# Moving a triangular inverse into the recurrence of a hybrid DeltaNet block, and re-laying its multipliers

## The chip, the cores and the metric

The kernel runs on one core of one Trainium2 chip. The metric is the device time of one execution in microseconds; the time before is the median of three runs. One execution was also recorded by the profiler.

## The reference

One layer of a bidirectional encoder block on 512 tokens of 1024 features in float32. What matters here is the gated DeltaNet branch and, at its edge, the rotary keys of the attention branch:

```python
def chunk_gated_delta_rule(q, k, v, g, beta):      # 8 heads of 128, chunks of 64
    ...
    lower = jnp.where(strict, jnp.einsum('bhnik,bhnjk->bhnij', k_beta, kc) * decay, 0.0)
    t_inv = lax.linalg.triangular_solve(eye + lower, ...)      # inverse of a unit lower triangle, 64 x 64
    u = t_inv @ v_beta
    w = t_inv @ (k_beta * jnp.exp(gc)[..., None])
    ...
    def step(state, xs):
        v_new = u_i - w_i @ state
        o_i = qd_i @ state + intra_i @ v_new
        state = state * jnp.exp(gl_i)[..., None, None] + jnp.swapaxes(ks_i, -1, -2) @ v_new
        return state, o_i
    _, o = lax.scan(step, state0, xs)

qkv = silu(conv(h @ w_in[:, :3072]))               # then heads, q and k normalised
o = o_fwd + o_bwd                                  # the rule once on the sequence, once on it reversed
k_rope = apply_rope(k_r, cos, sin)                 # k_r: 64 features shared by all attention heads
```

The block also has latent attention, a gated merge, an output projection, and an expert-choice mixture of 16 experts, of whose weights the second half of the time is spent streaming.

## The kernel before, in words

Float32 products are made on TensorE from halves: `split` (line 98) lets ScalarE round a tile to a high half, and VectorE or GpSimd subtracts it to get the low half; three matmuls of 128x512 then stand for one product. `lo_engine` (line 141) gives every `lo_n[0]`-th weight tile's low half to VectorE and the others to GpSimd: every third at first, every sixth in the value projection, every second in the recurrence. A projection tile has 24 such matmuls.

A scheduler fixes the order of instructions on each engine at compile time, from the order in which the code is written and from its own costs; every engine then runs its queue in that order and waits where an operand is missing.

The part of the program that the change touches runs like this:

1. *Latent projections and rotary keys* (lines 286 to 410). TensorE projects `kr_ps` (64 rotary features and 32 gate columns), ScalarE copies it to `kr1`, and a product with two identities doubles the 64 rows to 128 (`twice`). Sums of squares of the latent queries (`ones` against `sqs`) are copied to `rs`, transposed, and give the softmax scale `scq`. `rope` rotates the doubled keys: high half `rx`, low half `rl`, a permutation by TensorE into `pT`.
2. *Key and query projection*, then for four token tiles the decay matrices and the chunk products `gkq`; these give the strict triangles `nA` for both types of pass (ty 0 and 1).
3. *Inverses* (line 772). For each type, eight 32x32 diagonal blocks per lane set are gathered by way of memory (`nd_d`), one matrix per partition. `nl` holds the multipliers, `T` (named lanT in the trace) the inverse. Row i needs one multiply of i x i elements into `pr` (line 791) and one reduction (line 792), both on VectorE, for i from 1 to 31. The multipliers of a row are a column of `nl`: `n3[:, 0:i, i]`, a stride of 32 elements. Four copies then order the result (lines 794 to 797) and two stores send it to memory (`td_d`, `tt_d`).
4. *Value projection* (lines 801 to 811). Eight tiles (h = 0 to 7), alternating two PSUM banks `pja` and `pjb`, each followed by a filler tile of the output gates (PSUM tile `mm`). Of each value tile VectorE makes a convolution of four operations (lines 666 and 668), ScalarE the silu into `sl` (tile sq), and TensorE four transposes (`to_tok`, line 674, PSUM tile `tok`). The first inverse is written ahead of this loop; the second, which is written in step 2, is drawn up into it by the scheduler.
5. *Recurrence* (lines 816 to 950): eight steps of both directions at once, steps 0 to 3 with ty 0, steps 4 to 7 with ty 1. `level(s + 1)` loads the next step's blocks (`Tbd`, `TtC`, `vtok`, `ktok`, `kq`) through SP's queue and completes the 64x64 inverse with small corner products (`I<-TtC,Mb`, `I<-Tbd,Qb`). `step(s)` has for each group g of four heads the products Y and Q of the state, the subtraction of Y from `vtok` (line 900), the product V with the inverse, its scaling into `vtok` (line 915, VectorE), the state update S (line 933), and the output (lines 940 to 945). What is left of the 24 filler tiles fills TensorE in and behind the steps.
6. *Mixing* (from line 1005): norms of the outputs, transposes `oT`, output projections; then the experts.

Step 2 of the recurrence starts the second inverse in the code:

```python
for s in range(8):
    if s == 2:
        inverses(1)
    Ln = level(s + 1) if s < 7 else None
    step(s, L)
```

Of the kernel before, what the change touches and what calls it, by code (L numbers as in the profile page):

```python
# [14 lines left out]
OP = mybir.AluOpType  # L15
# [25 lines left out]
def block_kernel(ctx: ExitStack, tc: tile.TileContext, x, c, positions, w_mod, b_mod, g_mix, w_in, conv_w,  # L41
# [41 lines left out]
    def bank(name, bufs=2, reg=None):  # L83

        return (reg or pmm)(name if reg else "mm", 512, bufs=bufs)
# [25 lines left out]
    ident = cst("ident", 128)  # L111
# [232 lines left out]
    for i in range(2):  # L344
        dve.tensor_copy(twice[:64, 64 * i:64 * i + 64], ident[:64, :64])
    kr_ps = bank("kr")
    mm(kr_ps, twice[:64], kr1[:64])
    ss = lat[0]
# [5 lines left out]
    for t in range(4):  # L354
        pe.transpose(ss[:, 128 * t:128 * t + 128], rs[:, 128 * t:128 * t + 128], ident)
    scq = mp("scq", 4)
# [4 lines left out]
    p0.close()  # L361
    pm = Region("pmla", space=PSUM)

    pos_i = mp("pos_i", 1024, I32, tag="qn", bufs=2)[:, :512]
# [411 lines left out]
    def inverses(ty):  # L776
        nl, pr, T = lan("nl", 1024), lan("pr", 1024), lan("lanT", 1024)
        for l0, r0, th, c0 in blocks(ty):
            sp.dma_start(lanes_ap(nd_d[ty], l0),
                         nA[ty][th][r0:r0 + 32].rearrange("p (th n) -> p th n", n=64)[:, :, c0:c0 + 32])  # L780
        sp.dma_start(pr, nd_d[ty])
        dve.tensor_copy(nl[0:64], pr[0:64])
        dve.tensor_copy(nl[64:128], pr[64:128][:, ::-1])
        pool.memset(T, 0.0)
        pool.memset(T[:, 0:1024:33], 1.0)
        sq3 = lambda v: v.rearrange("p (a b) -> p a b", a=32)
        T3, n3 = sq3(T), sq3(nl)
        for i in range(1, 32):
            pv = pr[:, :i * i].rearrange("p (a b) -> p a b", a=i)
            nb = n3[:, 0:i, i][:, None, :].to_broadcast([128, i, i])  # L790
            dve.tensor_tensor(pv, T3[:, 0:i, 0:i], nb, op=OP.mult)  # L791
            dve.tensor_reduce(T3[:, 0:i, i], pv, axis=AX.X, op=OP.add)  # L792
        To, Tt = pr, nl
        dve.tensor_copy(To[0:64], T[0:64])
        dve.tensor_copy(To[64:128], T[64:128][:, ::-1])
        dve.tensor_copy(sq3(Tt)[0:64], T3[0:64].rearrange("p a b -> p b a"))
        dve.tensor_copy(sq3(Tt)[64:128], T3[64:128].rearrange("p a b -> p b a")[:, ::-1, ::-1])
        sp.dma_start(td_d[ty], To)
        sp.dma_start(tt_d[ty], Tt)

    inverses(0)
    lo_n[0] = 6
    for h, ps in proj_tiles(range(2048, 3072, 256), to=lambda n: bank(n, 1, pp_)):
        sl = dp("sq", 512, bufs=4)
        for _ in range(0):
            next(mod_g, None)
        conv(ps, 16 + h, halves(sl))
        to_tok(sl, 1, h, ssq_k[:, :, h])
        for _ in range(FV):
            next(fill_g)  # L810
    pp_.close()
    wm.close()
# [70 lines left out]
    def step(s, L):  # L883
# [24 lines left out]
        for g in range(2):  # L908
# [4 lines left out]
            if s < 7:  # L913
                v_ = vtok[:, hs, :]
                dve.tensor_tensor(v_, pV, bt[:, ty, t, hs][:, :, None].to_broadcast([128, 4, 128]), op=OP.mult)
            vn = dp("vn", [4, 128], bufs=2)
            for h in range(4):
                act.activation(vn[:, h, :], pV[:, h, :], AF.Copy, scale=col(beta, 4 * g + h))
            vns.append(vn)
        for g in range(2):  # L920
            if s < 7:
# [12 lines left out]
        for g in range(2):  # L934
# [8 lines left out]
            else:  # L943
                dve.tensor_tensor(Qs[g], pI, Qs[g], op=OP.add)
                pool.tensor_tensor(oo, oo, Qs[g], op=OP.add)

    L = level(0)
    for s in range(8):
        if s == 2:
            inverses(1)  # L950
        Ln = level(s + 1) if s < 7 else None
        step(s, L)
        L = Ln
# [712 lines left out]
```

## Time and profile before

| what | value |
|---|---|
| median of three runs | 1320.24 us (1316.88 to 1322.08) |
| the profiled execution | 1318.83 us, span 1316.9 us |
| busy: TensorE / VectorE / ScalarE / GpSimd | 1232.7 (94%) / 683.2 (52%) / 473.9 (36%) / 307.7 us (23%) |
| mean granted TensorE clock | 0.974 |
| the chain that ended last | TensorE 67%, VectorE 18% (multiplies of line 791: 4%, reductions of line 792: 2%), DMA 6% |
| multiplies of line 791 | 62, 59.1 us |

The busy share is an average over stages. The time of one stage is read from the waits and timelines of that stage; a span is 1.9 us shorter than the execution's time. In the rows PE is TensorE, PEld its weight loads, DVE VectorE, ACT ScalarE, POOL GpSimd, SP the engine that issues most loads. Two matmul records may stand for one float32 matmul of small operands.

### The profile page before, as it was taken

The page shows a single profiled execution, that of the slowest core. Times are in us where ns is not written, and L with a number is a line of the kernel's source. Part 1 is how long each engine was busy: PE and PEld are TensorE (multiplying, and loading weights), DVE is VectorE, ACT ScalarE, POOL GpSimd, SP SyncE. Part 2 cuts the span into 40 slices and gives each one's busy share as a digit, 9 for nine tenths or more (in the row PEclk, how much of TensorE's full clock was granted, in tenths as well). Part 3 has the DMA queues.
Part 4 walks back from the last instruction along what each step waited for, and adds up shares of the span by engine and source line. Part 5 has one row for each costly group of instructions (what it writes and reads, how often), then busy time and mean ns, then how long its engine had stood idle before and what let it go on. Part 6 is the DMA issues. An engine that isn't in the chain of part 4 may idle for free.

```text
span 1316.9 us, 18274 instructions
## 1 busy us (share of the span) xinstructions
PE 1232.7 (94%) x6911; PEld 773.7 (59%) x6911; DVE 683.2 (52%) x1312; ACT 473.9 (36%) x986; POOL 307.7 (23%) x258
## 2 busy tenths in 40 slices
PE   5999999999997889999999999699999999999895
PEld 2767777666676666878877777443433343343233
DVE  4577777475779895535576766511321312222125
ACT  4355655456543334444542226520210120120103
POOL 2221210332542352434222242300300020020003
PEclk9989999999998988999999999799999999999998
DMA  9421222754363557767479682699999999999995
GB/s 347 123 62 41 77 84 71 229 172 142 121 184 98 167 138 205 217 201 214 161 238 339 215 323 113 254 372 420 420 421 420 421 419 420 421 421 420 421 415 191
DMA packets 153842, 333.82 MB, mean 253 GB/s; under 512 B 44864, under 2 KB 104462, under 8 KB 128794
## 3 DMA queue, kind: packets, MB, share of 16 engines
q1 hardware_dynamic: 130048, 308.75, 63.7%
q10 hardware_dynamic: 23370, 23.50, 5.7%
q8 instruction: 54, 0.88, 0.3%
q0 software_dynamic: 336, 0.41, 0.2%
q14 instruction: 34, 0.28, 0.1%
HBM read 308.42 MB, written 24.20 MB: 253 GB/s over the span
## 4 chain that ended last, share of the span: by engine, by line
PE 67%; DVE 18%; DMA 6%; ACT 3%; issue 2%; POOL 1%; DVEq 0%; ACTq 0%; POOLq 0%; SPq 0%
PE mm L88 23%; PE wg L88 8%; PE dnp L88 7%; PE wu L88 7%; DVE pr L791 4%; PE po L88 4%; DMA exw<-in_w_down_dram 3%; PE sc L88 3%; DVE lanT L792 2%; PE s L88 2%; PE I L88 2%; DMA exw<-in_w_gate_dram 2%; PE S L88 1%; DVE cv L666 1%; DVE cv L668 1%
## 5 line engine op out<-in xcount | busy, mean ns | idle before, releaser
L88 PE MATMUL mm<-hT,wh 128*128 128x512 f32 (+1 forms) x656 | 219.0, 411 | 1.5 <-DVE cv L668 0.7
L96 POOL TENSOR_TENSOR wl<-wraw,wh 128x512 fp32r<-128x512 f32 (+1 forms) x82 | 117.5, 1448 | 289.8 <-ACT wh L99 252.5
L88 PEld LDWEIGHTS mm<-hT,wh 128*128 128x128 f32 (+1 forms) x656 | 123.6, 192 | 40.8 <-issue 8.8
L99 ACT ACTIVATE wh<-wraw 128x512 fp32r<-128x512 f32 (+1 forms) x138 | 86.5, 649 | 141.6 <-PE mm L88 75.5
L88 PE MATMUL mm<-hT,wl 128*128 128x512 f32 (+1 forms) x328 | 132.7, 405 | 0.0
L88 PE MATMUL wg<-exw,xe 128*64 128x512 f32 x512 | 121.2, 600 | 2.9 <-DMA exw<-in_w_gate_dram 1.6
L88 PE MATMUL wu<-exw,xe 128*64 128x512 f32 x512 | 119.2, 605 | 1.3 <-DMA exw<-in_w_up_dram 1.3
L96 POOL TENSOR_TENSOR xl<-xs,xh 128x512 fp32r<-128x512 f32 x32 | 40.3, 1275 | 308.2 <-ACT xh L1366 308.2
L1523 DVE TENSOR_TENSOR ye<-dnp,gt 64x512 f32<-64x512 f32 x30 | 20.7, 689 | 133.4 <-PE dnp L88 117.4
L1464 DVE TENSOR_TENSOR xa<-sc,xa 128x512 f32<-128x512 f32 x56 | 38.5, 691 | 87.7 <-PE sc L88 87.7
L88 PEld LDWEIGHTS wu<-exw,xe 128*64 128x64 f32 x512 | 35.3, 138 | 65.5 <-issue 59.4
L88 PEld LDWEIGHTS mm<-hT,wl 128*128 128x128 f32 (+1 forms) x328 | 62.7, 191 | 16.5 <-issue 1.9
L88 PEld LDWEIGHTS wg<-exw,xe 128*64 128x64 f32 x512 | 33.5, 136 | 64.0 <-issue 54.7
L791 DVE TENSOR_TENSOR pr<-lanT,nl 128x1 f32<-128x1 f32 (+30 forms) x62 | 59.1, 953 | 1.7
L96 DVE TENSOR_TENSOR wl<-wraw,wh 128x512 fp32r<-128x512 f32 (+2 forms) x56 | 45.0, 811 | 25.3 <-ACT wh L99 25.1
L88 PE MATMUL po<-W,am 128*128 128x512 f32 x192 | 50.4, 406 | 0.8 <-DVE W L96 0.6
L88 PE MATMUL mm<-am,wh 128*128 128x512 f32 x128 | 41.2, 399 | 0.0
L88 PEld LDWEIGHTS po<-W,am 128*128 128x128 f32 x192 | 34.4, 188 | 11.1 <-issue 1.6
L666 DVE SCALAR_TENSOR_TENSOR cv<-mm,vecT,cv 128x510 f32<-128x510 f32 (+1 forms) x32 | 23.8, 744 | 33.0 <-ACT cv L662 32.7
L88 PE MATMUL mm<-oz,wh 128*128 128x512 f32 x128 | 40.5, 398 | 0.2 <-ACT wh L99 0.2
L1589 POOL TENSOR_TENSOR xa<-xa,late 128x256 f32<-128x256 f32 (+1 forms) x16 | 10.7, 707 | 123.8 <-DMA late<-in_g_final_dram 123.8
L88 PE MATMUL mm<-OG,xh 128*128 128x256 f32 x128 | 34.2, 304 | 2.8 <-DVE OG L1375 2.8
(597 smaller groups left out, 2407.2 us busy)
## 6 DMA issues: line engine op xcount, KB each, us to landing
exw<-in_w_gate_dram SPq DMA_DIRECT2D x64, 1024.0 KB
exw<-in_w_up_dram SPq DMA_DIRECT2D x64, 1024.0 KB
exw<-in_w_down_dram SPq DMA_DIRECT2D x63, 1024.0 KB
wraw<-in_w_in_dram SPq DMA_DIRECT2D x38, 512.0 KB
wm<-in_w_mod_dram SPq DMA_DIRECT2D x32, 512.0 KB
wraw<-in_w_in_dram ACTq DMA_DIRECT2D x16, 512.0 KB
xa<-in_w_mod_dram SPq DMA_DIRECT2D x16, 512.0 KB
kq<-kq_d SPq DMA_DIRECT2D x7, 1024.0 KB
```

The lines of the kernel that those rows point to most:

```text
L88: return pe.matmul(o, lhsT, rhs, start=start, stop=stop)
L96: eng.tensor_tensor(o, a, b, op=OP.subtract)
L99: act.activation(hi, src, AF.Copy)
L666: dve.scalar_tensor_tensor(cv[:, -s:], ps[:, :512 + s], w(d), cv[:, -s:], op0=OP.mult, op1=OP.add)
L668: dve.scalar_tensor_tensor(cv[:, :512 - s], ps[:, s:], w(d), cv[:, :512 - s], op0=OP.mult, op1=OP.add)
L791: dve.tensor_tensor(pv, T3[:, 0:i, 0:i], nb, op=OP.mult)
L792: dve.tensor_reduce(T3[:, 0:i, i], pv, axis=AX.X, op=OP.add)
L1464: dve.tensor_tensor(y[t][:, c:c + 512], ps, y[t][:, c:c + 512], op=OP.add)
L1523: dve.tensor_tensor(ye[o_, c], ps[64 * q:64 * q + 64, :], gt2[64 * q:64 * q + 64, c], op=OP.mult)
L1589: pool.tensor_tensor(y[t][:, cs], y[t][:, cs], gfin[:, cs], op=OP.mult)
```

## The change

- The multipliers are transposed when they are copied into `nl`, so that row i reads `n3[:, i, 0:i]`, contiguous elements. The reversed half of the lanes is reversed in both directions.
- `inverses` becomes a generator that yields after every row. The first is run through at its old place. The second is run to row 12 ahead of level 0 and then in six portions, one behind each group's `vtok` scaling in steps 0, 1 and 2: to rows 17, 20, 23, 26, 29 and the end.
- The transposes of value tile h are written after the convolution of tile h + 1.
- In the value projection `lo_n[0]` is 1000 instead of 6: GpSimd makes all low halves of weights there.
- The doubling of the rotary keys is put behind the transposes of the sums of squares.

```diff
-    kr_ps = bank("kr")
-    mm(kr_ps, twice[:64], kr1[:64])
     ss = lat[0]
     for i in range(4):
         mm(ss[32 * i:32 * i + 32], ones[:, 0:32], sqs[:, i])
...
     for t in range(4):
-        pe.transpose(ss[:, 128 * t:128 * t + 128], rs[:, 128 * t:128 * t + 128], ident)
+        turned_ = pe.transpose(ss[:, 128 * t:128 * t + 128], rs[:, 128 * t:128 * t + 128], ident)
...
     pm = Region("pmla", space=PSUM)
+    kr_ps = bank("kr")
+    with tc.issue_after(turned_.ins):
+        mm(kr_ps, twice[:64], kr1[:64])
...
         sp.dma_start(pr, nd_d[ty])
-        dve.tensor_copy(nl[0:64], pr[0:64])
-        dve.tensor_copy(nl[64:128], pr[64:128][:, ::-1])
+        sq3 = lambda v: v.rearrange("p (a b) -> p a b", a=32)
+        flip = lambda v: sq3(v).rearrange("p a b -> p b a")
+        dve.tensor_copy(sq3(nl)[0:64], flip(pr)[0:64])
+        dve.tensor_copy(sq3(nl)[64:128], flip(pr)[64:128][:, ::-1, ::-1])
...
         for i in range(1, 32):
             pv = pr[:, :i * i].rearrange("p (a b) -> p a b", a=i)
-            nb = n3[:, 0:i, i][:, None, :].to_broadcast([128, i, i])
+            nb = n3[:, i, 0:i][:, None, :].to_broadcast([128, i, i])
             dve.tensor_tensor(pv, T3[:, 0:i, 0:i], nb, op=OP.mult)
             dve.tensor_reduce(T3[:, 0:i, i], pv, axis=AX.X, op=OP.add)
+            yield i
...
         sp.dma_start(tt_d[ty], Tt)
+        yield 32
 
-    inverses(0)
-    lo_n[0] = 6
+    for _ in inverses(0):
+        pass
+    lo_n[0] = 1000
+    turn = []
     for h, ps in proj_tiles(range(2048, 3072, 256), to=lambda n: bank(n, 1, pp_)):
...
         conv(ps, 16 + h, halves(sl))
-        to_tok(sl, 1, h, ssq_k[:, :, h])
         for _ in range(FV):
             next(fill_g)
+        turn.append((sl, 1, h, ssq_k[:, :, h]))
+        if h:
+            to_tok(*turn[h - 1])
+    to_tok(*turn[7])
...
-                dve.tensor_tensor(v_, pV, bt[:, ty, t, hs][:, :, None].to_broadcast([128, 4, 128]), op=OP.mult)
+                done = dve.tensor_tensor(v_, pV, bt[:, ty, t, hs][:, :, None].to_broadcast([128, 4, 128]), op=OP.mult)
...
             vns.append(vn)
+            if s < 3:
+                with tc.issue_after(done.ins):
+                    upto_i(INV[s][g])
...
+    INV, inv = ((17, 20), (23, 26), (29, 32)), inverses(1)
+
+    def upto_i(n):
+        while next(inv) < n:
+            pass
+
+    upto_i(12)
     L = level(0)
     for s in range(8):
-        if s == 2:
-            inverses(1)
         Ln = level(s + 1) if s < 7 else None
```

TensorE's queue in the value projection before, where tile 4 (pja_3720) begins; tok_3665 from sq_3656 are the transposes of tile 3:

```order
L88 MATMUL mm_3682<-hT7_103,wh_3676 128x512 x2
L88 MATMUL mm_3682<-hT7_103,wl_3677 128x512
L88 MATMUL pja_3720<-hT0_96,wh_3714 128x512 x2
L88 MATMUL pja_3720<-hT0_96,wl_3715 128x512
L88 MATMUL pja_3720<-hT1_97,wh_3714 128x512 x2
L88 MATMUL pja_3720<-hT1_97,wl_3715 128x512
L88 MATMUL pja_3720<-hT2_98,wh_3714 128x512 x2
L674 MATMUL tok_3665<-ident_77,sq_3656 128x128 x4
L88 MATMUL pja_3720<-hT2_98,wl_3715 128x512
```

The same transposes in the changed kernel, tok_3781 from sq_3645; mm_3753 is the filler behind tile 4, and pjb_3798 is tile 5:

```order
L88 MATMUL mm_3753<-hT6_102,wl_3748 128x512
L88 MATMUL mm_3753<-hT7_103,wh_3747 128x512 x2
L88 MATMUL mm_3753<-hT7_103,wl_3748 128x512
L675 MATMUL tok_3781<-ident_77,sq_3645 128x128 x4
L88 MATMUL pjb_3798<-hT0_96,wh_3792 128x512 x2
L88 MATMUL pjb_3798<-hT0_96,wl_3793 128x512
```

The transposes of tile 3 moved from the eighth matmul of tile 4 to the end of the filler behind tile 4.

VectorE's queue before, from the end of the second inverse to step 2 of the recurrence:

```order
L797 COPY nl<-lanT 64x1024
L96 TENSOR_TENSOR wl<-wraw,wh 128x512 x2
L915 TENSOR_TENSOR vtok<-V,bt 128x512 x2
L900 SCALAR_TENSOR_TENSOR vtok<-Y,negc,vtok 128x128 x8
L915 TENSOR_TENSOR vtok<-V,bt 128x512 x2
L933 TENSOR_TENSOR Sst<-Sst,S 128x4x128 x4
L942 TENSOR_TENSOR o_2024<-I,o_2024 128x512 x2
```

VectorE's queue now, from the second `vtok` scaling of step 1 on; pr and lanT are the second inverse:

```order
L924 TENSOR_TENSOR vtok<-V,bt 128x512
L793 TENSOR_TENSOR pr<-lanT,nl 128x529
L945 TENSOR_TENSOR Sst<-Sst,S 128x4x128
L794 TENSOR_REDUCE lanT<-pr 128x23
L945 TENSOR_TENSOR Sst<-Sst,S 128x4x128
L793 TENSOR_TENSOR pr<-lanT,nl 128x576
L945 TENSOR_TENSOR Sst<-Sst,S 128x4x128
L794 TENSOR_REDUCE lanT<-pr 128x24
L945 TENSOR_TENSOR Sst<-Sst,S 128x4x128
L793 TENSOR_TENSOR pr<-lanT,nl 128x625
L954 TENSOR_TENSOR o_2024<-I,o_2024 128x512
L794 TENSOR_REDUCE lanT<-pr 128x25
```

The multiplies and reductions of rows 13 to 31, which stood in one run ahead of the steps, now alternate with the state additions of steps 0 to 2.

TensorE's queue at the rotary keys before, and then now:

```order
L88 MATMUL lat_107<-sqs,ones 32x512
L88 MATMUL mm<-kr_616,twice 128x512
L88 MATMUL lat_107<-sqs,ones 32x512 x3
L88 MATMUL mm<-cq_492,uqh 128x512 x2
L88 MATMUL mm<-cq_492,uql 128x512
```

```order
L88 MATMUL lat_107<-sqs,ones 32x512 x4
L353 MATMUL lat_108<-ident,rs 128x128 x4
L88 MATMUL mm<-kr_616,twice 128x512
L88 MATMUL mm<-cq_492,uqh 128x512 x2
L88 MATMUL mm<-cq_492,uql 128x512
```

The doubling moved behind the other three sums and the four transposes of `rs`, which stood some eleven matmuls later.

## Rows read from the trace of the kernel before

**Rows 1.** Busy times by stretch: engines' busy us (instructions), granted clock, DMA share, GB/s.
```profile
374.10:507.50 133.40, 116.39 (x569) 91.39 (x568) 121.55 (x173) 51.13 (x117) 54.05 (x42) 0.94 0.52 150
507.50:528.00 20.50, 17.49 (x181) 13.94 (x179) 6.25 (x11) 10.07 (x28) 3.59 (x5) 0.83 0.80 225
528.00:636.00 108.00, 106.45 (x1291) 87.86 (x1290) 49.09 (x108) 49.98 (x169) 46.03 (x39) 1.00 0.68 197
```

**Rows 2.** Waits of TensorE from 360 to 520: total us, times, longest.
```profile
PE tok L674 <- ACT sq L669: 16.1, 5, 4.8
PE S L88 <- DVE vtok L915: 2.9, 1, 2.9
```

**Rows 3.** Timeline of TensorE, value projection: start, us, instruction, idle before and its releaser.
```profile
418.03 1.12 PE L674 MATMUL tok<-ident,sq 128*128 128x128 f32 x4 [3.65 <-ACT sq L669]
...
419.37 1.05 PE L88 MATMUL pja<-hT,wh 128*128 128x512 f32 x2
...
454.64 0.63 PE L88 MATMUL mm<-hT,wh 128*128 128x512 f32 x2
...
455.35 0.63 PE L88 MATMUL mm<-hT,wh 128*128 128x512 f32 x2
```

**Rows 4.** Timeline of VectorE, both inverses.
```profile
438.43 1.99 DVE L791 TENSOR_TENSOR pr<-lanT,nl 128x961 f32<-128x961 f32 x1
...
447.89 0.68 DVE L96 TENSOR_TENSOR wl<-wraw,wh 128x512 fp32r<-128x512 f32 x1
...
502.40 3.01 DVE L791 TENSOR_TENSOR pr<-lanT,nl 128x961 f32<-128x961 f32 x1
505.45 1.16 DVE L792 TENSOR_REDUCE lanT<-pr 128x31 f32<-128x961 f32 x1
...
508.14 1.21 DVE L796 COPY nl<-lanT 64x1024 f32<-64x1024 f32 x1
```

**Rows 5.** Groups of VectorE's instructions by line, 374 to 528: busy us, mean ns, idle before.
```profile
L791 DVE TENSOR_TENSOR pr<-lanT,nl 128x1 f32<-128x1 f32 (+30 forms) x62 | 59.1, 953 | 1.7
L792 DVE TENSOR_REDUCE lanT<-pr 128x1 f32<-128x1 f32 (+30 forms) x62 | 31.2, 502 | 1.7
```

**Rows 6.** Timeline of VectorE, end of the first inverse, start of the second.
```profile
445.28 1.12 DVE L797 COPY nl<-lanT 64x1024 f32<-64x1024 f32 x1
...
450.98 0.68 DVE L782 COPY nl<-pr 64x1024 f32<-64x1024 f32 x1 [1.15 <-DMA pr<-nd]
```

**Rows 7.** Timeline of GpSimd around 502.
```profile
500.74 2.89 POOL L96 TENSOR_TENSOR wl<-wraw,wh 128x512 fp32r<-128x512 f32 x2 [10.11 <-ACT wh L99]
```

**Rows 8.** The page's groups: a ScalarE pass of 512 columns, busy us, mean ns.
```profile
L99 ACT ACTIVATE wh<-wraw 128x512 fp32r<-128x512 f32 (+1 forms) x138 | 86.5, 649 | 141.6 <-PE mm L88 75.5
```

**Rows 9.** Groups of VectorE's instructions in the steps, 505 to 640.
```profile
L900 DVE SCALAR_TENSOR_TENSOR vtok<-Y,negc,vtok 128x128 f32<-128x128 f32 x56 | 15.8, 344 | 23.5 <-PE Y L88 23.1 <-DMA Tbd<-td 0.3
L933 DVE TENSOR_TENSOR Sst<-Sst,S 128x512 f32<-128x512 f32 x24 | 15.5, 684 | 8.3 <-PE S L88 8.2
```

**Rows 10.** Timeline of TensorE: the first V of steps 1 and 3.
```profile
527.96 0.94 PE L88 MATMUL V<-vtok,Tbd 128*128 128x128 f32 x6
...
558.77 0.71 PE L88 MATMUL V<-vtok,Tbd 128*128 128x128 f32 x4
```

**Rows 11.** Timeline of VectorE behind the steps.
```profile
635.89 0.69 DVE L944 TENSOR_TENSOR Qs<-I,Qs 128x512 f32<-128x512 f32 x1 [1.38 <-POOL o L945]
...
646.73 1.60 DVE L96 TENSOR_TENSOR am<-a__6088,am 128x512 fp32r<-128x512 f32 x1 [5.52 <-ACT am L99]
...
667.06 1.22 DVE L1040 TENSOR_TENSOR o<-o,ssq 128x1024 f32<-128x1024 f32 x1
```

**Rows 12.** Timeline of TensorE behind the steps.
```profile
672.62 1.03 PE L1045 MATMUL oT<-ident,o 128*128 128x128 f32 x8
```

**Rows 13.** Timeline of TensorE at the rotary keys.
```profile
78.86 2.07 PE L88 MATMUL mm<-kr,twice 64*128 64x512 f32 x2 [2.32 <-ACT kr L340]
```

**Rows 14.** Waits of SP's queue, 440 to 545: total us, times, longest.
```profile
SPq L836 <- DMA z_d<-zz: 27.1, 2, 16.3
```

More of the change, by code (lines that the diff above doesn't have):

```diff
@@ L781, in inverses @@
         sp.dma_start(pr, nd_d[ty])
-        dve.tensor_copy(nl[0:64], pr[0:64])
-        dve.tensor_copy(nl[64:128], pr[64:128][:, ::-1])
+        sq3 = lambda v: v.rearrange("p (a b) -> p a b", a=32)
+        flip = lambda v: sq3(v).rearrange("p a b -> p b a")
+        dve.tensor_copy(sq3(nl)[0:64], flip(pr)[0:64])
+        dve.tensor_copy(sq3(nl)[64:128], flip(pr)[64:128][:, ::-1, ::-1])
         pool.memset(T, 0.0)
         pool.memset(T[:, 0:1024:33], 1.0)
-        sq3 = lambda v: v.rearrange("p (a b) -> p a b", a=32)
         T3, n3 = sq3(T), sq3(nl)
```

## The prediction, made before the result was known

> **What bounds the kernel now.** I read busy times by stretch first. From 374.1 us, where the value projection's second tile starts, to 528.0, where step 1 of the recurrence begins, TensorE idles 17.0 + 3.0 us while VectorE is busy 121.6 of the first 133.4; from 528 to 636 TensorE idles only 1.6 of 108 and VectorE is less than half busy [rows 1]. So the cover is in the steps and the shortage in the value projection. TensorE's waits there have one name: 16.1 us in five waits of the value transposes for the silu, and 2.9 us of step 0's state product S for vtok, queued on VectorE behind the second inverse [rows 2]. Its timeline shows that a wait costs more than itself: after the wait of 3.65 us a pair of 512-wide matmuls takes 1.05 us instead of 0.63, the lower level of the granted clock (1.2 instead of 2.4 GHz) [rows 3]. The mean granted clock was 0.94 and 0.83 in the two stretches: (1 - 0.94) x 133.4 + (1 - 0.83) x 20.5 = 11.5 us at most. **The ceiling of the gain is 20.0 + 11.5 = 31.5 us.** TensorE was full in the next stretch, so time saved here is passed on.
>
> **Contiguous multipliers.** A multiply of 961 elements whose second operand strides by 32 takes 1.99 us; the reduction over the same count takes 1.16, and a two-input subtraction of contiguous operands 0.68 for 512, which is 1.28 for 961 [rows 4]. So the stride costs 0.71 to 0.83 us in 961, or 0.74 to 0.86 ns an element. One inverse multiplies 1 + 4 + ... + 961 = 10,416 elements: 7.7 to 9.0 us less; I take 8.3 (28% of the 59.1 / 2 = 29.6 us that one inverse's multiplies take [rows 5]). Against it stand two copies that now transpose: 1.21 instead of 0.68 each [rows 4, 6], 1.0 us. Four low-half subtractions of 0.68 [rows 4], which overlap a little, leave VectorE between 384 and 450: 2.5 us. VectorE thus passes the point it reached at 449.8 about 9.8 us earlier, near 440. GpSimd takes them at 1.45 us [rows 7]; one tile gives it two, 2.9 us per 5.6 us of TensorE, so it keeps up.
>
> **Value transposes a tile later.** Three matmuls start 0.71 us after one another's three, so one is 0.235 us [rows 3]. By the queue, the transposes of tile 3 stood 32 matmuls behind the tile's last one, 7.5 us; now it is 72, 16.9 us. The same 9 to 11 us of slack come to tiles 2 to 6; the longest wait is 4.8 [rows 2]. Only tile 7 keeps its place: 34 matmuls before, 35 now. Whether it waits depends on VectorE. If TensorE loses nothing, the queue puts tile 6's transposes at 374.1 + 80.8 = 454.9 and tile 7's at 457.8. VectorE finishes the first inverse's copies about 437; the second inverse's load lands 4.5 us later, as it did (446.4 to 451.0 [rows 6]), at 441.5. Then come two copies (2.3), rows 1 to 8 of the inverse with tile 6's convolution (7.3, to 451.1), rows to 12 and tile 7's convolution (4.4, to 455.5). Two silu passes of about 0.65 us [rows 8] end at 452.4 and 456.8, before 454.9 and 457.8. The margin at tile 7 is 1.0 us; one multiply that meets GpSimd costs as much (below). I leave 1 us (0 to 4).
>
> **The second inverse in the steps.** Rows 13 to 31 now stand on VectorE behind vtok of steps 0 to 2. By reductions of the trace (15.6 us for 31 rows [rows 5], 13 of them for rows 13 to 31) and multiplies at the contiguous price, portions are 7.7 us in step 0, 9.3 in step 1, and 10.8 plus four copies of 3.8 in step 2. In step 0 ScalarE copies the states, and only vtok needs VectorE. Steps 1 and 2 decide. One step's own work on VectorE is eight scaled subtractions at 0.28, two vtok products, four state additions and two output additions at 0.64 to 0.69 [rows 9]: 7.6 us, and 1.3 of low halves. Two steps with 9.3 and 14.6 us of inverse make 41.7. TensorE took 30.8 us from V of step 1 to V of step 3 [rows 10]; its queue now holds 60 projection matmuls there instead of 21, so 30.8 + 39 x 0.235 = 40.0. VectorE overruns by 1.7, and my walk through both queues finds two waits of V (1.0 and 1.4): 2.4 us. GpSimd adds to that: the last multiply took 3.01 instead of 1.99 [rows 4] while GpSimd's low halves ran [rows 7]; GpSimd is busy 43% of the steps [rows 1], and 11 multiplies lie there: 11 x 0.43 x 0.7 = 3.3. I take 5.5 us (0 to 12), with 2 us (0 to 5) for the lower clock behind such waits.
>
> **Behind the steps.** The projection matmuls spent in the steps are missing after them: 113 instead of 158 stand ahead of the output transposes, 26.5 us instead of 37. The chain there, from the last Qs addition at 635.89 to the last scaling of o that ends at 668.3, takes 32.4 us, of which 5.52 is one wait for ScalarE's am copies, themselves queued behind projection tiles [rows 11]; TensorE began the transposes at 672.62 [rows 12]. Without that wait it is 26.9. So there are 0 to 6 us of new wait; I take 1.5, since fewer projection tiles stand ahead of the copies.
>
> **Rotary keys.** TensorE waited 2.32 us for the copy of kr1, then doubled [rows 13]. Now the ones-sums and their transposes go first, but the copy rs, which they need, stands on ScalarE behind that same kr1 copy, and the rotation's first copy stands behind the ckv copies. The wait moves; between 2.3 gained and 2.3 lost I take 0.
>
> **Sum.** 31.5 - 1 - 5.5 - 2 - 1.5 - 0 = 21.5 us. The profiled execution took 1318.83 (span 1316.9), so 1297.3; the median of the runs is 1.4 above it: **1299 us**, a gain of 1.6%. Its own range is 1290 to 1306.
>
> **The rivals.**
> *GpSimd blocks the multiplies.* What happened at 502.40 happens to all of them: 11 multiplies by 1.02 us, 11.2 on top of 2.4 in steps 1 and 2, 5 for the clock and 3 behind the steps: 31.5 - 1 - 13.6 - 5 - 3 = 8.9, so 1311. For it: low halves left VectorE for GpSimd. Against it: GpSimd is under half busy there [rows 1]. The Trainium skill (SBUF — State Buffer, Who interferes with whom) says that a VectorE instruction with two SBUF inputs contends with a GpSimd instruction that reads SBUF, and that a reduction never does. The trace agrees: the multiply was 1.02 us longer, the reduction behind it, under GpSimd's next copies, kept its 1.16. By that rule each overlap is paid, which is this rival.
>
> *Loads set the start of the steps.* SP waited 27.1 us for writes of z before the TtC loads [rows 14]. If those loads don't move, V of step 0 waits about 10 us: 1309. Against it: the writes follow TensorE's projection tiles, which come earlier too, and TensorE waited for none of these loads.
>
> *The layout brings nothing.* If the 1.99 us are not the stride's, VectorE is 8.3 us later by tile 6 (8 us of waits with tile 7's) and 7.8 later in the steps, 5 for the clock: 31.5 - 8 - 13.3 - 5 - 1.5 = 3.7, so 1317. Against it: reductions of equal count.
>
> *Slower.* The second inverse goes onto the recurrence's path: SP holds its stores, and behind them kq, TtC and eight Tbd loads for steps 4 and 5. Its end moves from 510 to about 541. The corner product of step 4 stands some 20 us behind that in TensorE's queue, the stores and loads need about 10; from 10 us of further delay each microsecond is on the path. To end over 0.5% slower it takes 38 us in all, an inverse at more than twice its price: 1327. Against it: no row of the trace is that slow.
>
> **How the numbers follow.** Forecast 0.55, GpSimd 0.20, loads 0.10, layout 0.10, slower 0.05. A measurement of this kernel tells about 0.5% (6.6 us) from no change. The forecast and three quarters of the two next cases count as faster: 0.55 + 0.15 + 0.08 = 0.78, and 0.02 of the layout's case: 0.80. Same 0.15, slower 0.05. The range runs from the whole ceiling, 1289, taken as 1288, to 1314, which leaves out the last two cases and the tails of others.
>
> **What would show it.** Right: no wait of the value transposes over 2 us; the 961-element multiply at 1.15 to 1.3 us; V of step 0 near 485; one or two waits of V or Y for vtok in steps 2 and 3, a few microseconds in all; output transposes around 650. Wrong: multiplies still near 2 us; transposes of tile 7 waiting over 4 us; TensorE's waits in the steps above 12 us; V of step 0 waiting for Tbd or vtok loads.

## The result, and the profile after

The changed kernel takes **1306.02 us** (median of six runs, 1303.25 to 1306.68) against 1317.15 for the kernel before (six runs): a ratio of 0.9917 with a 95% interval from 0.9901 to 0.9933, so 0.7 to 1.0% faster. The forecast was 1299, the range 1288 to 1314. The two profiled executions are 13.3 us apart (1318.83 and 1305.51), and 21.5 had been forecast for that difference.

The stage is cut here at three events that both kernels have: the start of the value projection's second tile, the first V of the recurrence, the first output transpose. Of the kernel before, the first stretch is the first row of [rows 1]; the second is this (stretch, us, then busy us and instructions of TensorE, its weight loads, VectorE, ScalarE, GpSimd, then granted clock, DMA share, GB/s):

```profile
507.50:672.60 165.10, 160.54 (x1625) 131.17 (x1624) 78.31 (x186) 79.78 (x242) 59.12 (x50) 0.98 0.68 200
```

Both stretches of the change:

```profile
373.99:495.60 121.61, 114.45 (x546) 88.46 (x545) 80.19 (x132) 51.47 (x116) 56.72 (x46) 0.99 0.59 173
495.60:658.60 163.00, 157.13 (x1648) 128.06 (x1647) 105.05 (x223) 80.04 (x242) 62.25 (x50) 1.00 0.65 197
```

TensorE executes the same 2194 matmul records in both kernels, in 298.5 us before and in 284.6 now. Its idle time fell from 17.0 + 4.6 = 21.6 us to 7.2 + 5.9 = 13.0, its busy time from 276.9 to 271.6. So 8.6 us come from waits and 5.4 from shorter busy time, at a higher granted clock (0.99 and 1.00 instead of 0.94 and 0.98), 13.9 in all; the output transposes start at 658.6 instead of 672.6, and 13.2 are left at the end. What TensorE still waits for in the change, from 374 to 700 (us, times, longest):

```profile
PE mm L88 <- POOL wl L96: 3.7, 4, 1.3
PE mm L88 <- ACT wh L99: 2.1, 2, 1.7
PE Y L88 <- DMA kq<-kq_d: 2.1, 2, 1.4
PE V L88 <- DVE vtok L909: 1.1, 1, 1.1
...
PE oT L1063 <- DVE zo L1069: 0.7, 1, 0.7
...
PE tok L675 <- ACT sq L670: 0.6, 1, 0.6
```

The waits of the value transposes are gone (0.6 us where [rows 2] show 16.1), and so is the one of S for vtok. In their place are waits that the kernel before hardly had: 3.7 + 2.1 us for the low and high halves of weight tiles in the value projection, and 2.1 for the kq loads in the steps. VectorE's multiplies and reductions, from 374 to 600:

```profile
L793 DVE TENSOR_TENSOR pr<-lanT,nl 128x1 f32<-128x1 f32 (+30 forms) x62 | 43.7, 704 | 1.6
L794 DVE TENSOR_REDUCE lanT<-pr 128x1 f32<-128x1 f32 (+30 forms) x62 | 31.1, 502 | 1.5
```

Against [rows 5] the multiplies take 15.4 us less and the reductions the same. The chain of the page, by engine, now reads:

```profile
PE 34%; DMA 22%; DVE 4%; ACT 2%; issue 1%; POOL 0%; SPq 0%; DVEq 0%; ACTq 0%; POOLq 0%
```

This can't be set beside the chain before (TensorE 67%, VectorE 18%). In the change the chain was followed back only to 481.6 us, so its shares add up to 63%, and the value projection, where much of VectorE's share lay before, isn't in it. Of the DMA's 22%, 18 are expert weights. Where the bound went is read from the waits above.

### The profile page after: what moved, and what is told of

Same layout as the page of the kernel before. It is cut to its first block, busy times and chain, and to the rows that moved or that the text cites. A ratio compares the mean times of both kernels' runs of the same rounds, so it can differ in the third digit from the quotient of the medians.

```text
span 1303.7 us, 18255 instructions
## 1 busy us (share of the span) xinstructions
PE 1225.3 (94%) x6911; PEld 767.0 (59%) x6911; DVE 668.7 (51%) x1306; ACT 473.4 (36%) x986; POOL 314.5 (24%) x264
## 4 chain that ended last, share of the span: by engine, by line
PE 34%; DMA 22%; DVE 4%; ACT 2%; issue 1%; POOL 0%; SPq 0%; DVEq 0%; ACTq 0%; POOLq 0%
PE mm L88 11%; DMA exw<-in_w_down_dram 8%; DMA exw<-in_w_gate_dram 6%; PE wg L88 5%; DMA exw<-in_w_up_dram 4%; PE dnp L88 3%; PE wu L88 3%; PE po L88 2%; PE sc L88 2%; PE I L88 2%; PE Y L88 1%; DMA kq<-kq_d 1%; PE Q L88 1%; PE S L88 1%; DMA wraw<-in_w_o_dn_dram 1%
## 5 line engine op out<-in xcount | busy, mean ns | idle before, releaser
L96 POOL TENSOR_TENSOR wl<-wraw,wh 128x512 fp32r<-128x512 f32 (+1 forms) x88 | 126.8, 1457 | 254.8 <-ACT wh L99 236.9
L88 PE MATMUL wg<-exw,xe 128*64 128x512 f32 x512 | 121.8, 602 | 3.8 <-DMA exw<-in_w_gate_dram 2.5
L96 DVE TENSOR_TENSOR wl<-wraw,wh 128x512 fp32r<-128x512 f32 (+2 forms) x50 | 40.0, 811 | 39.5 <-ACT wh L99 28.9
L793 DVE TENSOR_TENSOR pr<-lanT,nl 128x1 f32<-128x1 f32 (+30 forms) x62 | 43.7, 704 | 1.6
```

The source lines that it names most:

```text
L88: return pe.matmul(o, lhsT, rhs, start=start, stop=stop)
L96: eng.tensor_tensor(o, a, b, op=OP.subtract)
```

## The experiments

Twelve kernels ran in three groups, each against its own runs of the kernel before. The first group undoes one part of the change at a time, the second does one part alone (and undoes the fifth), the third combines two parts; two kernels, one each in the second and third group, start the second inverse elsewhere. "Idle" is TensorE's, ahead of the first V (from the second value tile's start) and from there to the output transposes, in us of the profiled execution.

| kernel | median | ratio to before (95%) | first V | output transposes | idle |
|---|---|---|---|---|---|
| the change | 1306.02 | 0.9917 (0.9901 to 0.9933) | 495.6 | 658.6 | 7.2 + 5.9 |
| change, strided multipliers | 1320.89 | 1.0034 (1.0020 to 1.0048) | 504.5 | 670.5 | 12.1 + 8.4 |
| change, second inverse in one run | 1308.40 | 0.9930 (0.9916 to 0.9945) | 502.0 | 661.7 | 11.2 + 1.9 |
| change, every sixth low half on VectorE | 1303.97 | 0.9887 (0.9869 to 0.9905) | 491.2 | 655.7 | 3.7 + 7.4 |
| change, transposes at their old place | 1317.01 | 1.0001 (0.9988 to 1.0013) | 503.4 | 671.4 | 12.6 + 5.6 |
| change, rotary keys at their old place | 1306.53 | 0.9913 (0.9893 to 0.9933) | 497.6 | 661.0 | 7.3 + 6.2 |
| before + contiguous multipliers | 1300.05 | 0.9870 (0.9849 to 0.9891) | 496.6 | 655.9 | 10.0 + 1.8 |
| before + later transposes | 1317.76 | 1.0003 (0.9990 to 1.0015) | 507.5 | 669.9 | 17.9 + 4.7 |
| contiguous + all low halves on GpSimd | 1312.39 | 0.9961 (0.9946 to 0.9976) | 503.8 | 665.5 | 15.2 + 3.8 |
| contiguous + portions | 1306.53 | 0.9919 (0.9899 to 0.9939) | 493.3 | 659.8 | 7.2 + 5.5 |
| contiguous + later transposes | 1298.28 | 0.9856 (0.9836 to 0.9877) | 494.1 | 653.3 | 9.0 + 1.7 |
| second inverse behind tile 7 | 1295.25 | 0.9836 (0.9812 to 0.9860) | 486.0 | 647.5 | 1.0 + 2.0 |
| the same, transposes at their old place | 1305.07 | 0.9902 (0.9882 to 0.9922) | 495.6 | 661.2 | 8.6 + 4.7 |

### One part undone

**The layout.** The change with the strided copies and `n3[:, 0:i, i]` back:

```diff
-        dve.tensor_copy(sq3(nl)[0:64], flip(pr)[0:64])
-        dve.tensor_copy(sq3(nl)[64:128], flip(pr)[64:128][:, ::-1, ::-1])
+        dve.tensor_copy(nl[0:64], pr[0:64])
+        dve.tensor_copy(nl[64:128], pr[64:128][:, ::-1])
...
-            nb = n3[:, i, 0:i][:, None, :].to_broadcast([128, i, i])
+            nb = n3[:, 0:i, i][:, None, :].to_broadcast([128, i, i])
```

> The change with the multipliers left strided again. Theory (the stride costs VectorE 7 to 8 us an inverse, and a late VectorE now holds back the silus and the weights' high halves behind them): the 62 multiplies go back from about 46 to 59 us, the convolutions of tiles 3 to 7 end up to 8 us later, TensorE's idle time from 374 us to the first V rises from 7 to about 13 us, the steps lose some 3 more: 1316. Rival (the layout brings nothing, the gain is that of the transposes and the portions): 1306, within 2.

The multiplies went back to 59.6 us, the idle time ahead of the first V rose from 7.2 to 12.1, and the kernel is slower than the one before (1.0034, interval 1.0020 to 1.0048), and slower than the theory's 1316. The rival falls. So the other four parts together cost time unless the layout pays for them.

**The portions.** The change without `upto_i`, with the second inverse at its old place:

```diff
-            if s < 3:
-                with tc.issue_after(done.ins):
-                    upto_i(INV[s][g])
...
     for s in range(8):
+        if s == 2:
+            for _ in inverses(1):
+                pass
```

> The change with the second inverse written in one run at its old place, so drawn up ahead of step 0. Theory (VectorE is idle for some 28 of the 32 us between the last value convolution and V of step 0, so most of the second inverse fits there): the inverse ends near 497, V of step 0 stays near 496, its vtok scaling waits for a few us at most; the steps are freed: 1303 to 1311, 1307 likeliest. Rival (the portions carry the gain: VectorE holds the S of step 0 as before): a wait of 8 us or more at S of step 0, 1315.

1308.40, and the interval overlaps the change's. The steps became 3.3 us shorter (159.7 instead of 163.0 from the first V to the output transposes) and the value stage 5.0 longer, so the first V came at 502.0 and not near 496. No wait of S in step 0 came back. The wait that did appear stands in the value projection, with another name:

```profile
PE tok L675 <- ACT tk L681: 4.7, 1, 4.7
```

The transposes of tile 7 now wait for ScalarE to empty the PSUM tile of tile 6. ScalarE copies it (tk) in its own queue, where the silu of tile 7 waits for VectorE, whose queue holds the second inverse.

**The low halves.**

```diff
-    lo_n[0] = 1000
+    lo_n[0] = 6
```

> The change with every sixth low half of the value projection given to VectorE again. Theory (TensorE waits for the weights' halves because ScalarE's rounding stands behind silus that wait for VectorE): the waits of 6.1 us for wl and wh stay between 4 and 8, and four low halves on VectorE add up to 3: 1306 to 1309. Rival (GpSimd alone is too slow for the low halves): those waits fall below 2.5, 1302.

The theory falls here: the waits for weights' halves dropped to 2.4 us (it said 4 to 8, the rival under 2.5), and the time ahead of the first V went from 121.6 to 115.1 us. The total gained less: 1303.97, with an interval that overlaps the change's, since the steps took 1.5 us more (164.5, with 3.6 us of waits for kq) and the stage began later.

```profile
PE Y L88 <- DMA kq<-kq_d: 3.6, 2, 2.2
...
PE mm L88 <- POOL wl L96: 1.7, 2, 1.1
...
PE mm L88 <- ACT wh L99: 0.7, 1, 0.7
```

**The transposes.**

```diff
         conv(ps, 16 + h, halves(sl))
+        to_tok(sl, 1, h, ssq_k[:, :, h])
         for _ in range(FV):
             next(fill_g)
-        turn.append((sl, 1, h, ssq_k[:, :, h]))
-        if h:
-            to_tok(*turn[h - 1])
-    to_tok(*turn[7])
```

> The change with each tile's transposes written ahead of the filler again. Theory (the later transposes take the wait for the silu off TensorE, but what is behind it, the weights' halves, catches up to half of it): waits of tok of 6 to 10 us in the value projection, fewer for weights' halves, 1310. Rival (with contiguous multipliers VectorE is early enough anyway): waits of tok below 3 us, 1305.

The waits are as the theory had them (10.6 us of tok in five waits), the time is not: 1317.01, all of the gain is gone. Beside the waits, one matmul waited 1.8 us for a high half at 382 and the first inverse began late, at 393.06 against 388.33 in the change. The low halves account for much of that: with every sixth on VectorE and the transposes at their old place (contiguous + portions, below) the time is 1306.53.

**The rotary keys** were put back in a run of the second group:

```diff
-    kr_ps = bank("kr")
-    with tc.issue_after(turned_.ins):
-        mm(kr_ps, twice[:64], kr1[:64])
...
+    kr_ps = bank("kr")
+    mm(kr_ps, twice[:64], kr1[:64])
     ss = lat[0]
```

> The change with the rotary keys doubled at their old place again. Theory (the wait for ScalarE's copy only changes its name, 2.3 us for kr1 before, 3.1 to 3.7 for rs now): 1306, within 1.5. Rival (the later doubling gains the 2.3 us): 1308.5.

1306.53: no difference that these runs can tell. In the change the wait of 2.32 us for kr1 [rows 13] has become one of 3.09 us for rs:

```profile
78.60 0.71 PE L353 MATMUL lat<-ident,rs 128*128 128x128 f32 x4 [3.09 <-ACT rs L350]
```

### One part alone

**Contiguous multipliers alone**, the first diff of this section the other way round, on the kernel before:

> The kernel before with the contiguous multipliers alone. Theory (both parts are needed: with the transposes in their old place most of the wait for the silu comes back, as the run with the transposes put back showed with 10.6 us): waits of tok of 9 to 13 us instead of 16.1, no wait of S in step 0, 1312, between 1309 and 1316. Rival (the parts add: undoing the layout cost 15 us, so doing it gains as much): 1302.

Both expectations were off, and the rival was nearer: **1300.05, a ratio of 0.9870 (0.9849 to 0.9891), faster than the whole change.** The waits of tok are as the theory said, 7 us less than before:

```profile
PE tok L674 <- ACT sq L669: 9.1, 6, 3.1
```

Against the kernel before, TensorE's idle time ahead of the first V fell by 7.0 us and its busy time by 4.6, and behind it by 2.8 and 3.0. Why the steps gained is seen in VectorE's queue. The second inverse, in one run ahead of step 0, now ends just in time for the first V:

```profile
494.31 1.11 DVE L799 COPY nl<-lanT 64x1024 f32<-64x1024 f32 x1
495.45 1.50 DVE L96 TENSOR_TENSOR wl<-wraw,wh 128x512 fp32r<-128x512 f32 x2
497.72 0.69 DVE L917 TENSOR_TENSOR vtok<-V,bt 128x512 f32<-128x512 f32 x1 [0.77 <-DMA Tbd<-td]
```

VectorE is idle for 0.77 us ahead of vtok, TensorE waits nowhere for it, and the steps are free of the inverse: 159.3 us to the output transposes.

**Later transposes alone**, with the strided multipliers:

> The kernel before with the later transposes alone. Theory (VectorE stays late, so TensorE's wait goes to the next things that hang on it, weights' halves and the vtok scaling of step 0 behind the second inverse at about 510): tok waits below 3 us, but 8 us or more of waits for wh, wl and vtok together, 1315, between 1311 and 1319. Rival (the transposes alone carry the gain): 1306.

1317.76, no gain, as the theory said. The 16.1 us of waits for the silu became waits for everything else that hangs on the late VectorE:

```profile
PE tok L674 <- ACT tk L680: 9.4, 1, 9.4
PE mm L88 <- DVE wl L96: 3.9, 3, 1.9
...
PE mm L88 <- ACT wh L99: 2.5, 1, 2.5
```

### The second inverse behind the last value tile

In the change VectorE is idle for 28 of the 32.5 us between the last value convolution (465.0) and the first vtok scaling (497.5), with only a few low halves between, while rows 1 to 12 of the second inverse stand earlier, around the convolution of tile 6 and ahead of that of tile 7. This version puts rows 1 to 24 behind the last convolution and leaves the rest to the steps (every sixth low half on VectorE):

```diff
-    INV, inv = ((17, 20), (23, 26), (29, 32)), inverses(1)
+    INV, inv = ((25, 26), (28, 29), (31, 32)), inverses(1)
...
-    upto_i(12)
+    with tc.issue_after(last_cv[0].ins):
+        upto_i(24)
...
-    lo_n[0] = 1000
+    lo_n[0] = 6
```

> The change with every sixth low half on VectorE again, and the second inverse started behind the convolution of value tile 7: rows 1 to 24 there, then 25, 26, 27 to 28, 29, 30 to 31 and the copies in the steps. Theory (VectorE is idle between the last value convolution and V of step 0, and rows of the second inverse ahead of tiles 6 and 7 hold up silus and so the weights' halves): waits for wl and wh at most 1.5 us instead of 2.4 with the same low halves, V of step 0 near 489 instead of 491, fewer waits in the steps, 1300 to 1302. Rival (these waits don't hang on the second inverse, or its rows now stand in front of the vtok scaling of step 0): 1304 or more.

**1295.25, 0.9836 (0.9812 to 0.9860): better than both kernels.** Its two stretches and its waits from 372 to 700:

```profile
374.36:486.00 111.64, 110.61 (x547) 88.22 (x546) 91.42 (x159) 50.68 (x115) 50.42 (x41) 1.00 0.64 185
486.00:647.50 161.50, 159.47 (x1648) 130.24 (x1647) 92.71 (x199) 79.78 (x243) 60.89 (x50) 1.00 0.67 199
```

```profile
PE oT L1066 <- DVE zo L1072: 1.4, 1, 1.4
...
PE mm L88 <- POOL wl L96: 0.7, 1, 0.7
```

TensorE idles 1.0 us ahead of the first V, at full clock, and 2.0 behind it; V starts at 486.0, which is what the forecast wanted of the change (485). The theory's 1300 to 1302 was too high. The waits for kq are gone too: the second inverse is done in VectorE's queue some 21 us earlier (its stores are issued at 532.59 and 533.85 instead of 553.00 and 555.23), and the kq load behind it is issued at 544.37 instead of 557.65. Compared with the run that has the same low halves, only the place of the second inverse differs, and the median fell from 1303.97 to 1295.25; the two intervals do not touch. Its interval does overlap that of contiguous multipliers with later transposes (0.9836 to 0.9877, below), which leaves the second inverse in one run: that this place is better than that one isn't shown.

### Two parts together

Between contiguous multipliers alone (1300) and the change without its later transposes (1317) lie the portions and GpSimd's low halves. Each was added alone to the contiguous multipliers.

**All low halves on GpSimd** (`lo_n[0] = 1000` in place of 6):

> Contiguous multipliers and all low halves of the value projection on GpSimd, the rest as before. The change without its later transposes took 1317, the contiguous multipliers alone 1300; between them lie the portions and GpSimd's low halves. Theory (both cost: with GpSimd alone the first V comes 7 us later, as it did there): 1306, between 1303 and 1309. Rival (GpSimd's low halves cost the 2 us that they cost in the change, the portions all of the rest): 1302.

1312.39: it takes back 12 us, more than either expectation. Part of this is an order of ScalarE's queue that nobody wrote. At the second value tile ScalarE's queue with every sixth low half on VectorE, and then with all on GpSimd:

```profile
377.49 0.62 ACT L99 ACTIVATE wh<-wraw 128x512 fp32r<-128x512 f32 x1
379.18 1.15 ACT L680 ACTIVATE tk<-tok,ssq_k 128x128 f32<-128x128 f32 x4 [1.07 <-PE tok L674]
```

```profile
378.78 1.14 ACT L680 ACTIVATE tk<-tok,ssq_k 128x128 f32<-128x128 f32 x4 [0.75 <-PE tok L674]
379.80 0.64 ACT L99 ACTIVATE wh<-wraw 128x512 fp32r<-128x512 f32 x1
```

A weight tile's high half (wh) stood ahead of the copies of tok and stands behind them now. TensorE waits 1.75 us for it and 0.61 for the low half behind it, the convolution of that tile ends late, and the first inverse begins at 390.49 instead of 387.07. The waits of tok grew to 11.9. Where the transposes come later, this costs less: some 2 us in the change, by medians whose intervals overlap.

**The portions** (the `upto_i` lines of the change):

> Contiguous multipliers and the second inverse in portions, the rest as before. Theory (the portions cost in the steps: 168 us from the first V to the output transposes in the change without later transposes, 159 with the contiguous multipliers alone, with waits of Y for the kq loads behind the second inverse's stores): the first V at 494 to 497, 1306, between 1303 and 1309. Rival (they cost all of the 17 us): 1313 or more. Second rival (they cost nothing by themselves): 1300.

1306.53, as the theory had it: they cost 6.5 us. The stretch to the first V became 2.5 us shorter than with the contiguous multipliers alone (119.3 instead of 121.8), the one behind it 7.2 longer (166.5 instead of 159.3). Of those 7.2, 3.7 are idle time; TensorE's busy time there is 161.0 instead of 157.6 at the same granted clock. Its single matmuls take as long: the 224 of S have a mean of 293 ns in both runs, yet they cover 23.6 us instead of 22.1. So in that order of the queue neighbouring matmuls overlap less; what sets the overlap stays open. The waits for kq that the theory named did not come in this run; the cost came as waits for vtok, Sst, vn and o.

**The later transposes** on contiguous multipliers:

> Contiguous multipliers and the later transposes, the rest as before, so the second inverse is one run ahead of step 0. Theory (the waits change their name while VectorE's queue holds the second inverse ahead of tiles 6 and 7): 5 to 9 us of waits for tk, wh, wl and vtok in place of 9.1 for sq, 1301, between 1298 and 1305. Rival (the later transposes take the 9.1 us away here): 1291.

1298.28: 1.8 us less than without, and the intervals overlap. The 9.1 us of waits for sq became one wait of 6.9 for tk, as in the run with the second inverse in one piece. So the rival falls while the second inverse stands ahead of tile 7.

**The best version with the transposes at their old place:**

> The version of 1295 (contiguous, second inverse behind the last value convolution, every sixth low half on VectorE) with the transposes put back ahead of the filler. Theory (the waits of tok during the first inverse, some 6 us of the 9.1, have nothing to do with the second inverse and come back): 1300, between 1298 and 1303. Rival (with VectorE early the place of the transposes is of no account): 1295, within 1.5.

1305.07, worse than the theory's 1298 to 1303, and the rival falls: with the second inverse out of the way the later transposes are worth 10 us. Only 4.7 us of tok waits returned; 2.0 us for low halves on VectorE and 2.8 + 1.7 at V for vn and the vtok load came with them.

## Why the prediction was right in its sign, and what took half of the gain

**What bounds the kernel: right.** The shortage of VectorE in the value projection was the bound. One edit that only makes its multiplies cheaper brought 1.3%.

**The ceiling: nearly right.** The fastest stretches of these runs put the work of the 2194 records at about 268.5 us of busy time (the change with every sixth low half on VectorE: 111.4 + 157.2). Against this the kernel before lost 21.6 us idle and 8.4 in longer busy time, at granted clocks of 0.94 and 0.98, 30.0 in all, where the text had 31.5. Its clock term, 11.5, also counted the low clock during waits, in which no matmul is slowed.

**Contiguous multipliers: right.** Forecast 0.74 to 0.86 ns an element and 16.6 us in both inverses; measured 15.4 (59.1 to 43.7). The 961-element multiply takes 1.17 us in the first inverse with contiguous multipliers alone; in the change it is 2.02 and 2.28, for the reason in the last section:

```profile
431.80 2.02 DVE L793 TENSOR_TENSOR pr<-lanT,nl 128x961 f32<-128x961 f32 x1
...
546.41 2.28 DVE L793 TENSOR_TENSOR pr<-lanT,nl 128x961 f32<-128x961 f32 x1
```

A row of 400 elements shows the stride best (mean of two; the kernel before, then contiguous multipliers alone, and the reduction of the same 400):

```profile
L791 DVE TENSOR_TENSOR pr<-lanT,nl 128x400 f32<-128x400 f32 x2 | 1.7, 866 | 0.0
```

```profile
L793 DVE TENSOR_TENSOR pr<-lanT,nl 128x400 f32<-128x400 f32 x2 | 1.1, 569 | 0.0
L794 DVE TENSOR_REDUCE lanT<-pr 128x20 f32<-128x400 f32 x2 | 1.1, 565 | 0.0
```

(866 - 569) / 400 = 0.74 ns an element, and a contiguous multiply costs what a reduction costs. The Trainium skill (SBUF — State Buffer, Door 1: The DMA port swizzle, in its note on cachelines) says that accesses within one 16-byte line run at full rate and that each new line costs extra; a stride of 32 float32 elements touches a new line each time, and this trace agrees in the direction.

**Value transposes a tile later: the step that failed.** "If TensorE loses nothing, the queue puts tile 6's transposes at 374.1 + 80.8 = 454.9", "I leave 1 us (0 to 4)". They came at 465.0, and the stage lost 10.2 us: 7.2 idle and 3.1 of longer busy time (121.61 us in all, against the 111.38 that TensorE is busy with this work in the run with every sixth low half on VectorE). The working asked only whether silus are in time for transposes, and closed the low halves with "one tile gives it two, 2.9 us per 5.6 us of TensorE, so it keeps up". GpSimd has the time on average, but its input comes late. Around 457 us in the change, ScalarE, GpSimd and TensorE:

```profile
455.78 0.72 ACT L670 ACTIVATE sq<-cv 128x256 f32<-128x256 f32 x2 [8.81 <-DVE cv L669]
456.40 0.61 ACT L99 ACTIVATE wh<-wraw 128x512 fp32r<-128x512 f32 x1
```

```profile
457.15 1.27 POOL L96 TENSOR_TENSOR wl<-wraw,wh 128x512 fp32r<-128x512 f32 x1 [7.14 <-ACT wh L99]
```

```profile
457.07 0.73 PE L88 MATMUL mm<-hT,wh 128*128 128x512 f32 x2 [1.70 <-ACT wh L99]
458.48 0.80 PE L88 MATMUL mm<-hT,wl 128*128 128x512 f32 x1 [0.68 <-POOL wl L96]
459.07 1.06 PE L88 MATMUL mm<-hT,wh 128*128 128x512 f32 x2
...
465.02 0.60 PE L675 MATMUL tok<-ident,sq 128*128 128x128 f32 x4
```

ScalarE sat 8.81 us in front of the silu that VectorE had not yet fed; the next weight tile's high half stood behind it, GpSimd, idle for 7.14 us, made the low half behind that, and TensorE waited for both, with pairs at the lower clock after (1.06 us, as in [rows 3]). With a sixth of the low halves on VectorE the two waits shrink to 0.73 and 0.64 us and those ahead of them are gone (idle 3.7 in the stage); with the second inverse out of the way of tiles 6 and 7 as well, these two are gone too (idle 1.0).

**The second inverse in the steps: about the right size, the wrong place.** Forecast 5.5 + 1.5 us of new waits there and behind, with 2 for the clock; the change idles 5.9 us from the first V on, at full clock, and V did wait once for vtok (1.1). But 2.1 us are waits for kq, which the text had only in its slower rival, behind the stores of the second inverse. SP's queue in the change and what it waited for from 485 to 600, then VectorE and TensorE:

```profile
553.00 0.33 SPq L801 DMA_DIRECT2D td<-pr  x1
555.23 0.33 SPq L802 DMA_DIRECT2D tt<-nl  x1
557.65 0.32 SPq L863 DMA_DIRECT2D kq<-kq_d  x1
```

```profile
SPq L863 <- PE Y L88: 9.2, 2, 7.2
```

```profile
554.12 1.08 DVE L800 COPY nl<-lanT 64x1024 f32<-64x1024 f32 x1
555.24 0.87 DVE L909 SCALAR_TENSOR_TENSOR vtok<-Y,negc,vtok 128x128 f32<-128x128 f32 x3
```

```profile
555.64 0.49 PE L88 MATMUL V<-vtok,Tbd 128*128 128x128 f32 x2 [1.13 <-DVE vtok L909]
...
556.51 1.09 PE L88 MATMUL Y<-Sst,kq 128*64 128x128 f32 x16
...
564.83 0.84 PE L88 MATMUL Y<-Sst,kq 128*64 128x128 f32 x10 [1.36 <-DMA kq<-kq_d]
```

The stores don't hold the load: they had left by 555.6, and the load went out at 557.65, when Y of the running step had read the old block (kq has one buffer). That Y stood in TensorE's queue behind the V that waited for vtok, and the subtraction into vtok stood on VectorE behind the last copy of the inverse. The other wait for kq, 0.70 us at 538.97, came ahead of these stores, for a load issued at 532.71, again behind a Y. So the larger wait comes of VectorE's lateness in the steps, as the text had it, by a path that it did not name; the rival's mechanism did not show. What the text missed is that the move was not needed: with contiguous multipliers the whole second inverse ends at 495.4 and the first V comes at 496.6.

**Behind the steps and the rotary keys: right.** 0.7 us of wait at the output transposes (1.5 forecast, 0 to 6), and nothing for the keys (0 forecast).

**The sum again, by measured terms.** 30.0 - 10.2 (value stage) - 5.9 (from the first V on) = 13.9 us, the difference at the output transposes; the forecast's terms were 31.5 - 1 - 9 = 21.5. The value stage's term alone is off by 9.2. The sum also added 1.4 us, by which the median of three runs before lay above the profiled execution; with six runs the median before, 1317.15, lies 1.7 below it. That the time is still between 1288 and 1314 is owed to the width of that range: the forecast's own, 1290 to 1306, ends just below it.

**The rivals.** That the layout brings nothing is refuted by two runs. That loads set the start of the steps did not happen: the first V waited for nothing. GpSimd's blocking is real, yet it was no new cost: where a contiguous multiply costs what a reduction costs, the change's multiplies have 43.7 - 31.1 = 12.6 us on top, and the kernel before, less the stride's 2 x 10,416 x 0.74 ns = 15.4, had 59.1 - 31.2 - 15.4 = 12.5.

**Of the signs** that were named, the waits of tok below 2 us came, and one wait of V for vtok in step 3 (1.13 us); V of step 0 near 485 and the output transposes near 650 did not (495.6 and 658.6). The 961-element multiply was to take 1.15 to 1.3 us if the text was right and near 2 if it was wrong: it took 2.02 and 2.28, and yet the layout worked. The sign was a poor one, since GpSimd's hold on a multiply looks the same there as the stride.

What stays open: why the matmuls behind the first V overlap less in the run with portions, and how much of the 12 us of the low halves is the order of ScalarE's queue and how much GpSimd's speed. No run parted the two.

## What to carry to other kernels

Run each part of a change alone before you keep the whole: here one part gave 17 us, two of the others took back 12 and 6.5 when added to it, and the sum looked like a success. When an engine is late, removing a wait that hangs on it only renames the wait; list everything in every in-order queue that stands behind that engine's results, the other engines' queues included, before a wait is counted as gained. Before work is moved onto a recurrence, look for idle time of its engine ahead of it: 28 us of it lay between the last value tile and the first step.

## What the runs showed of the hardware that I had not expected

One GpSimd subtraction holds a VectorE multiply for as long as it runs, whatever the multiply's size. VectorE's first rows in the change, while GpSimd's queue ran two low halves from 389.45 to 392.00:

```profile
389.50 1.27 DVE L793 TENSOR_TENSOR pr<-lanT,nl 128x16 f32<-128x16 f32 x1
390.81 0.17 DVE L794 TENSOR_REDUCE lanT<-pr 128x4 f32<-128x16 f32 x1
391.01 1.03 DVE L793 TENSOR_TENSOR pr<-lanT,nl 128x25 f32<-128x25 f32 x1
392.07 0.18 DVE L794 TENSOR_REDUCE lanT<-pr 128x5 f32<-128x25 f32 x1
```

```profile
389.45 2.55 POOL L96 TENSOR_TENSOR wl<-wraw,wh 128x512 fp32r<-128x512 f32 x2 [3.31 <-ACT wh L99]
```

A multiply of 16 elements takes 1.27 us, 1.1 more than the mean of 0.18 in the run with the second inverse behind tile 7; the reductions in between (0.17 and 0.18) are not touched. The multiply of 961 elements loses no more by a meeting (2.02 instead of 1.17 us). So many small instructions suffer more than a few large ones, by the count of meetings. The Trainium skill (SBUF — State Buffer, Who interferes with whom) calls it an exclusive lock in which the later one blocks for the whole instruction, and the trace agrees. It also names copies that run in a two-port mode as taking part; the copy of 64x1024 at 435.05 took 1.72 us while GpSimd worked, and the one behind it 0.69:

```profile
435.05 1.72 DVE L797 COPY pr<-lanT 64x1024 f32<-64x1024 f32 x1
436.78 0.69 DVE L798 COPY pr<-lanT 64x1024 f32<-64x1024 f32 x1
```
